# Dummy products and dummy vector operations behind a two-stage attention kernel

## The chip, the cores and the metric

The kernel runs on one core of a Trainium2 chip. The metric is the device time of one execution in microseconds. Times of several executions are given by their median. One execution is recorded by the hardware profiler, and its span, from the first to the last instruction, is read beside the times.

The engines are named as in the profile: PE is TensorE's matrix product, PEld its weight load, DVE is VectorE, ACT is ScalarE, POOL is GpSimd and SP is SyncE, which here only issues transfers.

## The reference

One decoder layer on 256 rows of width 4096: a root-mean-square norm, one projection to q, k, v and a gate, stick-breaking attention with 32 heads of 128, the gate, a second projection, the residual, and a final norm. (The loop over layers runs once, so the convolution branch is not reached.)

```python
def attn_branch(xn, w_in, w_out):
    b, s, _ = xn.shape
    proj = xn @ w_in
    q, k, v, g = jnp.split(proj, 4, axis=-1)
    ...
    o = stick_breaking_attention(to_heads(q), to_heads(k), to_heads(v))
    o = o.transpose(0, 2, 1, 3).reshape(b, s, ATT_WIDTH)
    return (o * jax.nn.silu(g)) @ w_out
...
    h = h + attn_branch(rms_norm(h, norm_attn), w_in_attn, w_out_attn)
    ...
    return rms_norm(h, final_norm)
```

All arrays are float32. The products are the two projections, 256 x 4096 x 16384 and 256 x 4096 x 4096, and the small ones of the heads.

## The kernel before

**Splitting.** Every float32 weight tile `raw` (128 x 1024) is cut into a high half `wh`, made by a ScalarE copy to the type float32r, and a low half `wl`, the difference, made by a VectorE subtraction. The stationary operands are split the same way (`sh`/`sl`, `oh`/`ol`). One product in float32 precision is then three products in float32r (`mm3`): high by high, high by low, low by high. A product has 128 rows, 128 stationary columns and 512 moving columns, and the moving operand is always read in one contiguous run of 512.

**Blocks.** The output columns are taken in 20 units, 16 for the first projection and four for the second. A unit goes through 16 steps of two weight tiles. Steps in the list `SEVEN` use a scheme with seven products in place of eight, for which VectorE and an adding transfer on the POOL queue form sums of weight blocks in place. Results collect in PSUM banks `b1` to `b7`.

**Order.** The class `Plan` simulates the five engines with costs and due times and emits each instruction when its engine would be free; every instruction it emits goes through `keep_in_program_order` (line 121 in the profile, the line of a helper), so those of the kernel keep their order on each engine. Buffers are rings: seven `raw` tiles, five pairs `wh`/`wl` (tag `w`), two single pairs, three tiles `gh`.

**The end.** The products of the last five parts (`KEPT`) are ordered by bank, `LAST_ORDER = (5, 4, 2, 3)`, so that the banks are finished one after another. Behind each bank DVE adds it to the residual rows `h`, ACT squares them for the norm (`sq`), a Newton step gives the factor, and DVE and ACT scale the rows, which SP writes out.

```python
    for s in EIGHT_LAST:
        nc.start(again(s))
    nc.start(last_h())
    nc.run()
```

These are the last lines of the kernel; `nc.run()` lets the plan run out.

Of the kernel before, what the change touches and what calls it, by code (L numbers as in the profile page):

```python
# [10 lines left out]
F32 = mybir.dt.float32  # L11
F32R = mybir.dt.float32r
BF16 = mybir.dt.bfloat16
AF = mybir.ActivationFunctionType
ALU = mybir.AluOpType
# [4 lines left out]
P = 128  # L20
# [5 lines left out]
CW = 256  # L26
HG = CW // P
NB = D // CW
W = 2 * CW
NJ = D // W  # L30
KT = 2
# [11 lines left out]
RAW_BUFS = 7  # L43
PAIRS = 5
# [193 lines left out]
def kernel(  # L238
# [10 lines left out]
    nc = Plan(tc)  # L249
    scale = 1.0 / math.sqrt(P)  # L250

    cp = ctx.enter_context(tc.tile_pool(name="const", bufs=1))
    wp = ctx.enter_context(tc.tile_pool(name="weights", bufs=1))
    sp = ctx.enter_context(tc.tile_pool(name="stationary", bufs=1))
    dp = ctx.enter_context(tc.tile_pool(name="spill", bufs=1, space=DRAM))
    acc = ctx.enter_context(tc.tile_pool(name="acc", bufs=1, space=PSUM))
    att = ctx.enter_context(tc.tile_pool(name="att", bufs=1, space=PSUM))
    rooms = ExitStack()
    ap = rooms.enter_context(tc.tile_pool(name="attention", bufs=1))
# [38 lines left out]
    starts, ends, first, left, place_of = {}, {}, {}, {}, {}  # L298
    PRODUCT = 3 * tensor_ns(W)
    for g, (n, k) in enumerate(order):  # L300
        p = parts[n]
        b = p["u"], p["prods"][k][0]
# [51 lines left out]
    raw, wh, wl = {}, {}, {}  # L354
# [215 lines left out]
    for k in range(WARM):  # L570
# [10 lines left out]
        out=bound, in_=bound, compare_op=ALU.is_gt, fill=0.0, base=0,  # L581
# [6 lines left out]
        out=tri_f, in_=tri_f, compare_op=ALU.is_ge, fill=0.0, base=0, pattern=[[-1, P]], channel_multiplier=1,  # L588
# [465 lines left out]
    def last_h():  # L1054

        u, c = LAST, NJ - 2
        bank = ev.setdefault(u, {})
        key = place_of[u + 1, 0] - (KEPT * 4 + 8) * PRODUCT
        late = place_of[u + 1, 0]
        add = lambda to, f, g, k=late, n=W: dve(  # L1060
            lambda: nc.vector.tensor_tensor(out=to, in0=f, in1=g, op=ALU.add), n, k
        )
        for d in range(2):
            yield nc.until(("used", u, LAST_STEPS[d]))
            new_h(c + d)
        for d in range(2):
            yield nc.until(("used", u, LAST_STEPS[2 + d]))
            for t in range(NT):
                yield load_out(c + d, t)
        yield nc.until(("h", c - 1))  # L1070
        for d in range(2):
            yield nc.take("gh")
            yield load_gain(c + d)
        one, two = ([hs[c + d, t] for t in range(NT)] for d in range(2))
        yield nc.until(("full", u, 1))
        yield act(lambda: nc.scalar.copy(two[0], bank[1]), W, key)
        yield act(lambda: nc.scalar.copy(one[0], bank[1]), W, key)
        yield nc.until(("full", u, 6))
        yield add(two[0], bank[6], two[0], key)
        yield nc.until(("full", u, 7))  # L1080
        yield add(two[1], bank[7], two[0], key)
        yield act(lambda: nc.scalar.copy(one[1], two[1]), W, key)
        for t, b, d in ((1, 5, 1), (1, 4, 0), (0, 2, 0), (0, 3, 1)):
            nc.start(block_done(c + d, t, b, bank, add, key + 10 * (NT - 1 - t), late))
        yield nc.until("C22")
        yield add(two[0], bank[5], two[0], late - 1)
        nc.tell("C12")
# [148 lines left out]
        nc.start(again(s))  # L1236
    nc.start(last_h())
    nc.run()


# [36 lines left out]
```

## Time and profile before

| | us |
|---|---|
| median of 2 runs | 1739.97 (1739.81 to 1740.13) |
| span of the profiled execution | 1738.8 |
| PE busy | 1722.9 (99%) |
| DVE busy | 1643.5 (95%) |
| ACT busy | 1204.9 (69%) |
| POOL busy | 335.5 (19%) |

The profiled execution's own time is not listed beside its span; the runs lie 1.0 to 1.3 us above the span. Busy time of PE counts pipelined products whose shown lengths overlap: their starts, not their lengths, give the pace. In the timeline a row is the start in us, the length in us, the engine, the line, the operation and its operands as output<-inputs; in square brackets stands how long the engine was idle before it and what ended that wait. In the groups a row ends with the busy time, the mean length in ns, and the idle time before.

### The profile page before, as it was taken

To read this page: it belongs to the slowest core of one execution; us is meant where nothing else is said; L and a number is where in the kernel's file an instruction comes from. 1 tells how busy PE (TensorE), PEld (TensorE's weight loads), DVE (VectorE), ACT (ScalarE), POOL (GpSimd) and SP (SyncE) were. 2 spreads that over 40 slices of the span, in tenths; PEclk is the share of its full clock that TensorE was granted. 3 is DMA by queue.
4 is the path that set the end of the run, shared out by engine and by line. 5 is a ranking of instruction groups with operands and counts; after the bars stand their busy time and mean duration, and the time that the engine had idled before them with its cause. 6 is when DMAs were issued, how large, how long until landed. Compare 5 with 4: busy or idle time off the path is not lost.

```text
span 1738.8 us, 24830 instructions
## 1 busy us (share of the span) xinstructions
PE 1722.9 (99%) x7735; PEld 1412.5 (81%) x7735; DVE 1643.5 (95%) x2106; ACT 1204.9 (69%) x1640; POOL 335.5 (19%) x407
## 2 busy tenths in 40 slices
PE   9999999999999999999999999999999999999997
PEld 6888888888888888888888888888888888878885
DVE  8889999999999999999999999999999987999997
ACT  7976767676767676767676767676767675666655
POOL 0022222222222221212222222222222112221220
PEclk9999999999999999999999999999999999999999
DMA  9967788878787878787878787878787878788895
GB/s 363 297 191 227 229 231 226 230 229 236 224 234 223 240 216 238 217 251 208 255 206 255 206 256 198 257 203 259 198 256 203 269 245 265 230 268 251 233 303 191
DMA packets 249380, 413.79 MB, mean 238 GB/s; under 512 B 28128, under 2 KB 73440, under 8 KB 249248
## 3 DMA queue, kind: packets, MB, share of 16 engines
q1 hardware_dynamic: 194544, 354.24, 60.6%
q0 software_dynamic: 54416, 57.70, 20.2%
q8 instruction: 60, 0.98, 0.2%
q14 instruction: 72, 0.59, 0.1%
q10 hardware_dynamic: 288, 0.28, 0.0%
HBM read 403.98 MB, written 8.13 MB: 237 GB/s over the span
## 4 chain that ended last, share of the span: by engine, by line
PE 78%; DVE 12%; issue 6%; ACT 2%; DMA 2%; SPq 0%; DVEq 0%; ACTq 0%
PE acc L121 74%; DVE wl L121 8%; DVE raw L121 3%; PE z L121 2%; PE o L121 1%; ACT wh L121 1%; DMA raw<-in_w_in_dram 1%; PE tr L121 1%; DVE gv_sb L121 1%; DVE h L121 0%; DMA raw<-in_w_out_dram 0%; DMA grow<-in_gain_out_dram 0%; DVE qk_sb L121 0%; SPq L121 0%; ACT sq L121 0%
## 5 line engine op out<-in xcount | busy, mean ns | idle before, releaser
L121 ACT CAST wh<-raw 128x1024 fp32r<-128x1024 f32 (+1 forms) x995 | 922.0, 971 | 406.1 <-issue 180.0
L121 DVE TENSOR_TENSOR wl<-raw,wh 128x1024 fp32r<-128x1024 f32 (+1 forms) x995 | 1068.8, 1123 | 58.4 <-ACT wh L121 56.6
L121 PE MATMUL acc<-wh,sh 128*128 128x512 f32 x1898 | 755.6, 398 | 0.0
L121 PE MATMUL acc<-wl,sh 128*128 128x512 f32 x1898 | 740.0, 390 | 0.8 <-DVE wl L121 0.8
L121 PE MATMUL acc<-wh,sl 128*128 128x512 f32 x1898 | 740.5, 390 | 0.0
L121 POOL DMA_DIRECT2D raw<-in_w_in_dram x300 | 262.9, 988 | 1078.9 <-DMA raw<-in_w_in_dram 427.4
L121 PEld LDWEIGHTS acc<-wh,sl 128*128 128x128 f32 x1898 | 356.3, 188 | 75.8 <-DVE sl L121 0.4
L121 PEld LDWEIGHTS acc<-wl,sh 128*128 128x128 f32 x1898 | 357.0, 188 | 73.8 <-DVE wl L121 2.8
L121 PEld LDWEIGHTS acc<-wh,sh 128*128 128x128 f32 x1898 | 356.8, 188 | 70.7 <-ACT wh L121 0.6
L121 DVE TENSOR_TENSOR raw<-raw,raw 128x512 f32<-128x512 f32 x354 | 243.4, 687 | 6.9 <-DMA raw<-in_w_out_dram 1.2
L121 PE MATMUL acc<-wl,oh 128*128 128x512 f32 x485 | 189.7, 391 | 2.0 <-DVE wl L121 1.8
L121 PE MATMUL acc<-wh,oh 128*128 128x512 f32 x485 | 190.0, 392 | 0.0
L121 PE MATMUL acc<-wh,ol 128*128 128x512 f32 x485 | 188.9, 389 | 0.0
L121 DVE TENSOR_TENSOR raw<-raw 128x512 f32<-128x512 f32 x177 | 121.0, 684 | 0.0
L121 PEld LDWEIGHTS acc<-wl,oh 128*128 128x128 f32 x485 | 91.1, 188 | 23.8 <-DVE wl L121 5.3
L121 PEld LDWEIGHTS acc<-wh,oh 128*128 128x128 f32 x485 | 91.0, 188 | 19.2 <-DVE gv_sb L121 0.5
L121 PEld LDWEIGHTS acc<-wh,ol 128*128 128x128 f32 x485 | 91.0, 188 | 18.8
L121 POOL DMA_DIRECT2D raw<-in_w_out_dram x54 | 47.1, 968 | 185.9 <-DVE wl L121 58.9
L121 ACT ACTIVATE f<-f 128x384 f32<-128x384 f32 x96 | 50.5, 526 | 3.0
L121 ACT COPY qkT<-tr 128x512 f32<-128x512 f32 x32 | 18.6, 581 | 24.1 <-PE tr L121 24.1
L121 ACT CAST oh<-p 128x512 fp32r<-128x512 f32 (+3 forms) x46 | 20.9, 467 | 18.8 <-DVE p L121 13.2
L121 DVE SCALAR_TENSOR_TENSOR gv_sb<-acc,rin_v,gv_sb 128x512 f32<-128x512 f32 x45 | 33.4, 741 | 0.0
(91 smaller groups left out, 750.3 us busy)
## 6 DMA issues: line engine op xcount, KB each, us to landing
raw<-in_w_in_dram SPq DMA_DIRECT2D x1024, 256.0 KB, 4.5
raw<-in_w_out_dram SPq DMA_DIRECT2D x256, 256.0 KB, 4.3
raw<-in_w_in_dram POOLq DMA_DIRECT2D x300, 128.0 KB, 4.7
p<-spill POOLq DMA_DIRECT2D x28, 256.0 KB, 4.2
raw<-in_w_out_dram POOLq DMA_DIRECT2D x54, 128.0 KB, 5.1
xr<-in_x_dram SPq DMA_DIRECT2D x16, 256.0 KB, 4.8
xres<-in_x_dram SPq DMA_DIRECT2D x16, 256.0 KB, 5.6
out_dram<-h SPq DMA_DIRECT2D x16, 256.0 KB, 2.8
```

The source lines that it names most:

```text
L121: return self.tc.keep_in_program_order(getattr(self.engine, name)(*args, **kw))
```

## The change

Behind `nc.run()` a new function `probes` is called with the plain engine handle, not with the `Plan`, so its instructions are not held to the program order in the way that the kernel's are. Its tiles take places in the kernel's own rings: `zero`, `probe_f` and `probe_g` among the `raw` tiles, `probe_wh`, `probe_wl`, `probe_b`, `probe_r` and `probe_r2` among the pairs; the products write bank `b1`, and `probe_bank` is bank `b6`. All operands are zero, and nothing of it reaches the output.

```diff
     nc.start(last_h())
     nc.run()
+    probes(tc.nc, wp, acc)
+LANES = [
+    [(1, 512)],
+    [(16, 32), (1, 16)], [(4, 4), (16, 32), (1, 4)], [(4, 4), (20, 32), (1, 4)], [(4, 4), (12, 32), (1, 4)],
+    [(4, 4), (24, 32), (1, 4)], [(4, 4), (28, 32), (1, 4)], [(4, 4), (8, 32), (1, 4)], [(0, 4), (4, 32), (1, 4)],
+    [(8, 128), (1, 4)], [(0, 128), (1, 4)], [(0, 32), (1, 16)], [(0, 2), (1, 256)], [(0, 8), (1, 64)],
+    [(20, 32), (1, 16)], [(24, 32), (1, 16)], [(28, 32), (1, 16)], [(32, 32), (1, 16)],
+    [(256, 4), (8, 32), (1, 4)], [(128, 4), (4, 32), (1, 4)], [(256, 4), (6, 32), (1, 4)],
+    [(8, 2), (20, 32), (1, 8)], [(8, 2), (24, 32), (1, 8)], [(8, 2), (28, 32), (1, 8)], [(8, 64), (1, 8)],
+    [(12, 64), (1, 8)], [(16, 64), (1, 8)],
+    [(4, 4), (18, 32), (1, 4)], [(4, 4), (22, 32), (1, 4)], [(4, 4), (30, 32), (1, 4)],
+    [(48, 16), (1, 32)], [(40, 16), (1, 32)], [(36, 16), (1, 32)], [(64, 8), (20, 4), (1, 16)],
+    [(2, 2), (4, 128), (1, 2)], [(4, 2), (8, 64), (1, 4)], [(4, 8), (32, 16), (1, 4)], [(4, 2), (16, 64), (1, 4)],
+    [(256, 2), (4, 64), (1, 4)], [(12, 42), (1, 12)], [(20, 25), (1, 20)], [(24, 21), (1, 24)],
+]
+AGAIN = 12
+def probes(nc, wp, acc):
+    zero = wp.tile([P, HG, KT, CW], F32, tag="raw", name="zero", bufs=RAW_BUFS)
+    nc.vector.memset(zero, 0.0)
...
+    for t in (m, w, mb):
+        nc.scalar.copy(t, zero)
...
+    for n in (1024, 512, 256, 128):
+        for k in range(6):
+            tt(out=r2[:, 0:n], in0=zero[:, 0:n], in1=rf[:, 0:n], op=sub)
...
+    for k in range(6):
+        tt(out=f[:, 0:512], in0=zero[:, 0:512], in1=zero[:, 512:1024], op=sub)
...
+    for k in range(10):
+        tt(out=f[:, 0:512], in0=zero[:, 0:512], in1=zero[:, 512:1024], op=sub)
+        nc.gpsimd.tensor_tensor(out=g[:, 512:1024], in0=zero[:, 0:512], in1=zero[:, 512:1024], op=add)
+    for k in range(6):
+        nc.scalar.copy(r2, zero)
...
+    for dims in LANES:
...
+        for k in range(AGAIN):
+            one(lanes(m, dims), dims, n, w[:, 128 * (k % 2) : 128 * (k % 2) + 128], True)
+    for at_ in (2, 4, 8, 12, 16, 512):
+        for k in range(AGAIN):
+            one(m[:, at_ : at_ + 512], [(1, 512)], 512, w[:, 128 * (k % 2) : 128 * (k % 2) + 128], True)
+    for n in (480, 384, 256, 128, 64):
...
+    for k in range(AGAIN):
+        one(mb[:, 0:512], [(1, 512)], 512, mb[:, 128 * (k % 2) : 128 * (k % 2) + 128], True)
+    for k in range(AGAIN):
+        one(m[:, 0:512], [(1, 512)], 512, w[:, 0:64], True, to=out[0:64])
...
```

An entry of `LANES` lists the free dimensions of the moving operand from the outermost in, as (step in elements, count): `[(4, 4), (16, 32), (1, 4)]` reads runs of four elements, 32 of them 16 elements apart, and that four times, each time four elements further on. `lanes` builds the access pattern, and `one` issues the product. Each pattern is run 12 times with two stationary blocks in turn. Behind the patterns come six other offsets of a contiguous run, five smaller widths, and single groups with bfloat16 operands, with 64 stationary columns, with 64 rows, with one stationary column repeated, with the stationary operand out of the moving tile, and with accumulation. The groups of DVE, ACT and POOL repeat a subtraction, sum, copy or scaling six times (one of them ten), on the tiles named above.

More of the change, by code (lines that the diff above doesn't have):

```diff
@@ L1238, with lanes, one @@
     nc.run()
+    probes(tc.nc, wp, acc)
+LANES = [
[12 rows of a table added]
+]
[3 more added lines that the diff above has]
+    nc.vector.memset(zero, 0.0)
+    zero = zero.rearrange("p i k n -> p (i k n)")
+    m, w = (wp.tile([P, KT, W], F32R, tag=t, name=f"probe_{t}", bufs=PAIRS) for t in ("wh", "wl"))
+    mb = wp.tile([P, KT, W], BF16, tag="wh", name="probe_b", bufs=PAIRS)
+    m, w, mb = (t.rearrange("p k n -> p (k n)") for t in (m, w, mb))
+    for t in (m, w, mb):
+        nc.scalar.copy(t, zero)
+    out = acc.tile([P, W], F32, tag="b1", name="probe_out")
+    f = wp.tile([P, HG, KT, CW], F32, tag="raw", name="probe_f", bufs=RAW_BUFS).rearrange("p i k n -> p (i k n)")
+    g = wp.tile([P, HG, KT, CW], F32, tag="raw", name="probe_g", bufs=RAW_BUFS).rearrange("p i k n -> p (i k n)")
+    r = wp.tile([P, KT, W], F32R, tag="wh", name="probe_r", bufs=PAIRS).rearrange("p k n -> p (k n)")
+    r2 = wp.tile([P, KT, W], F32R, tag="wl", name="probe_r2", bufs=PAIRS).rearrange("p k n -> p (k n)")
+    bank = acc.tile([P, W], F32, tag="b6", name="probe_bank")
+    nc.scalar.copy(bank, zero[:, 0:W])
+    nc.scalar.copy(r, zero)
+    runs = lambda t: t.rearrange("p (h i e) -> p i h e", i=4, e=4)
+    cut = lambda t: t.rearrange("p (i h e) -> p i h e", i=4, e=4)
+    rf, mf = r.bitcast(F32), m.bitcast(F32)
+    tt, sub, add = nc.vector.tensor_tensor, ALU.subtract, ALU.add
+    for n in (1024, 512, 256, 128):
+        for k in range(6):
+            tt(out=r2[:, 0:n], in0=zero[:, 0:n], in1=rf[:, 0:n], op=sub)
+    for k in range(6):
+        tt(out=r2[:, 0:512].rearrange("p (h i e) -> p h i e", i=2, e=4), in0=zero[:, 0:512], in1=rf[:, 0:512], op=sub)
+    for k in range(6):
+        tt(out=f[:, 0:512], in0=zero[:, 0:512], in1=zero[:, 512:1024], op=sub)
+    for k in range(6):
+        tt(out=f[:, 0:512], in0=bank, in1=zero[:, 512:1024], op=sub)
+    for k in range(6):
+        tt(out=f[:, 0:512], in0=zero[:, 512:1024], in1=bank, op=sub)
+    for k in range(6):
+        nc.vector.tensor_scalar(out=f, in0=zero, scalar1=1.0, scalar2=None, op0=ALU.mult)
+    for k in range(6):
+        nc.vector.tensor_scalar(out=r2, in0=zero, scalar1=1.0, scalar2=None, op0=ALU.mult)
+    for k in range(6):
+        nc.vector.tensor_copy(r2, zero)
+    for k in range(6):
+        nc.vector.tensor_copy(f[:, 0:512], bank)
+    for k in range(6):
+        nc.gpsimd.tensor_tensor(out=g[:, 0:512], in0=zero[:, 0:512], in1=zero[:, 512:1024], op=add)
+    for k in range(6):
+        tt(out=f[:, 0:512], in0=g[:, 0:512], in1=zero[:, 512:1024], op=sub)
+    for k in range(10):
+        tt(out=f[:, 0:512], in0=zero[:, 0:512], in1=zero[:, 512:1024], op=sub)
+        nc.gpsimd.tensor_tensor(out=g[:, 512:1024], in0=zero[:, 0:512], in1=zero[:, 512:1024], op=add)
+    for k in range(6):
+        nc.scalar.copy(r2, zero)
+    for k in range(6):
+        nc.scalar.copy(f, zero)
+    for k in range(6):
+        nc.scalar.copy(r2[:, 0:512], bank)
+    for k in range(6):
+        nc.scalar.activation(f[:, 0:512], bank, AF.Copy, scale=1.0)
+    def lanes(t, dims, at_=0):
+        a = t[:, at_ : at_ + 1]
+        return bass.AP(tensor=a.tensor, offset=a.offset, ap=[a.ap[0], *([s, n] for s, n in dims)])
+    def one(moving, dims, n, still, first, rows=slice(0, P), to=None):
+        o = out[:, 0:n] if to is None else to
+        shape = [n_ for _, n_ in dims]
+        if len(shape) == 2:
+            o = o.rearrange("p (a b) -> p a b", b=shape[1])
+        if len(shape) == 3:
+            o = o.rearrange("p (a b c) -> p a b c", b=shape[1], c=shape[2])
+        nc.tensor.matmul(o, still, moving, start=first, stop=True, skip_group_check=True)
+    for dims in LANES:
+        n = 1
+        for _, c in dims:
+            n *= c
+        for k in range(AGAIN):
[5 more added lines that the diff above has]
+        for k in range(AGAIN):
+            one(m[:, 0:n], [(1, n)], n, w[:, 128 * (k % 2) : 128 * (k % 2) + 128], True)
+    for k in range(AGAIN):
+        one(mb[:, 0:512], [(1, 512)], 512, mb[:, 128 * (k % 2) : 128 * (k % 2) + 128], True)
+    for k in range(AGAIN):
+        one(m[:, 0:512], [(1, 512)], 512, w[:, 0:64], True, to=out[0:64])
+    for k in range(AGAIN):
+        one(m[0:64, 0:512], [(1, 512)], 512, w[0:64, 0:128], True)
+    for k in range(AGAIN):
+        one(m[:, 0:512], [(1, 512)], 512, w[:, 0:1].broadcast_to([P, P]), True)
+    for k in range(AGAIN):
+        one(m[:, 0:512], [(1, 512)], 512, m[:, 0:128], True)
+    for k in range(AGAIN):
+        one(m[:, 0:512], [(1, 512)], 512, w[:, 0:128], k == 0)
```

## The prediction

> **What bounds the kernel now.** I read the page first (busy shares, granted clock), then two stretches of the windows view, then the timeline of one undisturbed stretch for the pace of the products, then the timeline of the last 30 us.
>
> ```profile
> span 1738.8 us, 24830 instructions
> PE 1722.9 (99%) x7735; PEld 1412.5 (81%) x7735; DVE 1643.5 (95%) x2106; ACT 1204.9 (69%) x1640; POOL 335.5 (19%) x407
> PE  9999999999999999999999999999999999999997
> ...
> 1000.00:1100.00 100.00, 100.00 (x453) 82.34 (x452) 95.49 (x116) 68.23 (x89) 20.49 (x25) 1.00 0.80 230
> 1690.00:1727.00 37.00, 37.00 (x164) 30.32 (x162) 34.02 (x53) 20.69 (x35) 1.76 (x2) 1.00 0.58 181
> 1727.00:1738.00 11.00, 0.27 (x2) 0.00 (x0) 4.37 (x13) 3.46 (x9) 0.00 (x0) 0.68 0.81 303
> ```
>
> The columns of the windows are the stretch, its length, then PE, PEld, DVE, ACT and POOL, the granted clock, the DMA share and GB/s. TensorE works from beginning to end at clock 1.00, and only the last 11 us are without it. Its total idle time is 1738.8 - 1722.9 = 15.9 us. There is no hole into which more products could go, so whatever is put on PE behind the last product of the kernel lengthens the span by its own time, less the 11 us of tail that it covers.
>
> The pace of a product is read from starts, since a product's shown length (390 ns) overlaps the next one.
>
> ```profile
> 317.70 0.39 PE L121 MATMUL acc<-wh,sl 128*128 128x512 f32 x1
> ...
> 329.94 0.39 PE L121 MATMUL acc<-wh,sl 128*128 128x512 f32 x1
> ...
> 317.93 0.19 PEld L121 LDWEIGHTS acc<-wl,sh 128*128 128x128 f32 x1
> ...
> 302.29 0.22 PE L121 MATMUL z<-fh,neg_tri 128*128 128x128 f32 x1
> 302.35 0.27 PE L121 MATMUL z<-fl,neg_tri 128*128 128x128 f32 x1
> ```
>
> Between the first two rows lie 54 steps without a gap: 12.24 us / 54 = 226.7 ns for a product of 512 columns whose moving operand is read in one contiguous run. Each brings its own weight load, 190 ns long, hidden beside the product before. The last two rows show that a product of 128 columns can be followed by the next after 60 ns when its weights are there.
>
> The end of the kernel:
>
> ```profile
> 1710.71 0.68 DVE L121 TENSOR_TENSOR h<-h,grow 128x512 f32<-128x512 f32 x1
> 1711.45 2.36 DVE L121 TENSOR_TENSOR wl<-raw,wh 128x1024 fp32r<-128x1024 f32 x2
> 1713.73 1.41 DVE L121 TENSOR_TENSOR h<-acc,h 128x512 f32<-128x512 f32 x2
> 1715.06 1.22 DVE L121 TENSOR_TENSOR wl<-raw,wh 128x1024 fp32r<-128x1024 f32 x1
> 1716.32 0.19 PEld L121 LDWEIGHTS acc<-wl,oh 128*128 128x128 f32 x1 [0.30 <-DVE wl L121]
> ...
> 1726.88 0.39 PE L121 MATMUL acc<-wh,ol 128*128 128x512 f32 x1
> 1727.06 8.02 SPq L121 DMA_DIRECT2D out_dram<-h  x10
> ...
> 1731.30 1.41 DVE L121 SCALAR_TENSOR_TENSOR h<-h,factor,grow 128x512 f32<-128x512 f32 x2
> ...
> out_dram<-h SPq DMA_DIRECT2D x16, 256.0 KB, 2.8
> ```
>
> The last low half `wl` is finished at 1716.28, and PE waits 0.30 us for it: DVE has no slack there. The last product starts at 1726.88, DVE's last row ends at 1732.7, the last output is issued at 1735.1 and lands some 2.8 us later at 1737.9. The span closes 0.9 us after that. The median of the runs, 1739.97, lies 1.2 us above the profiled span, and I add the same 1.2 to the new one.
>
> **The change part by part.** Nothing is removed. `probes` is called after `nc.run()`, but the scheduler of the tile framework interleaves its VectorE and ScalarE instructions with the tail; only PE's stand strictly behind the last product. As built, PE gets 59 groups of 12, 708 products: 51 groups of 512 columns, two of 504, one each of 500, 480, 384, 256, 128 and 64. (42 of the groups are the list `LANES`; the rest vary offset, width, dtype and the stationary operand.)
>
> *PE, at the contiguous pace.* 612 products x 0.2267 = 138.7 us. The narrower ones by their share of the width: 24 x 0.2231 = 5.4, 12 x 0.2214 = 2.7, then 480, 384 and 256 columns 2.5 + 2.0 + 1.4 = 5.9. The 24 of 128 and 64 columns lie between the 60 ns above and the 190 ns of their weight load; I take 0.11, 2.6 us (ends 1.4 and 4.6). Together **155.3 us**. One bank receives all of them, but the kernel's own products also write one bank several times running at this pace, so I add nothing.
>
> [...]
>
> *PE, the patterns.* The trace holds no product whose moving operand is read in broken runs, so this cost is bounded from both sides. Below: the contiguous row, extra 0. Above: twice that row for each group that jumps after every four elements or fewer (strides 8 to 32, 6, 18, 22 and 30, repeats of four, and the one with runs of two). I count 17 such groups: 17 x 12 x 0.2267 = 46.2 us. Runs of 8, 16 and 32 are nearer to the contiguous row and I give them nothing. Of the two ends the value is nearer to the lower, because it is the only row of this instruction with this amount of data; but 17 patterns that differ so much will hardly all keep it. I take **10 us**, about what one group in four at half pace costs (4 x 2.72 = 10.9).
>
> *DVE ahead of the last product.* As built, a memset of 1024 elements stands three `wl` ahead of the last one, and two subtractions of 512 elements stand between that memset and the last `wl`.
>
> ```profile
> L121 DVE MEMSET idle<- 128x320 uint32 x10 | 3.2, 325 | 1.7 <-PEq L1264 0.9
> L121 DVE TENSOR_TENSOR wl<-raw,wh 128x1024 fp32r<-128x1024 f32 x816 | 957.1, 1219 | 57.1 <-ACT wh L121 55.4
> L121 DVE TENSOR_TENSOR h<-h,xres 128x512 f32<-128x512 f32 x16 | 10.7, 685 | 1.3 <-DMA xres<-in_x_dram 1.3
> ...
> L121 ACT CAST wh<-raw 128x1024 fp32r<-128x1024 f32 x816 | 825.5, 1049 | 335.5 <-issue 138.8 <-PE acc L121 127.6 <-DVE raw L121 55.3
> L121 ACT COPY gv_sb<-acc 128x512 f32<-128x512 f32 x15 | 8.7, 577 | 0.0
> ...
> L121 POOL TENSOR_SCALAR_AFFINE_SELECT tri_f<-tri_f 128x128 f32<-128x128 f32 x1 | 0.3, 295 | 0.1
> ```
>
> The memset by its row: 1024/320 x 325 = 1.04 us. The subtractions 2 x 0.6 (0.685 long, 0.08 of it overlapped). Together 2.2 us, ends 1.5 and 2.5. PE already waits 0.30 us for that `wl`, so nothing hides it: **+2.2 us** on the end of the kernel's own products. Queued behind them on DVE are also the last sums, but these no longer decide.
>
> *ACT ahead of the first dummy product.* It needs the copies `probe_wl` and `probe_wh` (1.05 us each by the `wh` row), and these need a buffer that the last five kept parts give back. Such buffers come free during the last products, and between the two copies stands a square that waits for DVE. Ends: 0, where both end ahead of the last product, and 1.3 us, where the second buffer is the last one freed. I take **+0.4 us**. The bf16 copy and `probe_r` follow long before they are read.
>
> *The other engines' 24 groups.* DVE: 46 subtractions of 512 x 0.685 = 31.5, six of 1024 x 1.22 = 7.3, the twelve narrower ones at no more than 0.685 = 8.2, eighteen copies or scalings of 1024 at no more than 1.22 = 22, six copies of a bank 4.1: 73 us. ACT behind the tail: 12 x 1.05 + 12 x 0.58 = 19.6 us, and it waits for DVE, whose results it overwrites. POOL: 16 sums of 512, no such row; by its 128-element row 1.2 us each, twice that for two inputs, 19 to 38 us. In series, DVE and then ACT: 1732.7 + 10 (tail pushed back) + 73 + 20 = 1836, and with POOL's upper end wholly added 1874. PE's dummies run until about 1895, so all this is worth **0**, with 20 us or more to spare; without that cover it would cost some 95 us. The kernel's own tail and its outputs, late by up to 10 us, lie under the same cover.
>
> **The sum.** End of the last product's slot 1726.88 + 0.23 = 1727.1; + 2.2 + 0.4 = 1729.7, where the dummies start; + 155.3 + 10 = 1895.0; the last one's length beyond the pace 0.2 and the close of the span 0.9: span 1896.1. With 1.2 around it: **1897 us**, 157 us or 9% above before. Against no change a measurement of this kernel tells about 2%, 35 us.
>
> **The rivals.**
>
> *Every pattern keeps the contiguous pace* (0.33): extra 0, 1897 - 10 = 1887 us. For it: at the contiguous pace PE takes 512 x 4 bytes per partition in 226.7 ns and nothing in the trace shows that reading is its limit. Against it: nothing shows that it is not, and 17 of 59 groups read only 8 or 16 bytes before a jump. [...]
>
> *Four-element runs halve the pace* (0.14): 1887 + 46 = 1933 us. For it speaks only that a jump per 16 bytes means 128 jumps in 226.7 ns. Against it: such a penalty would have to hold for odd and even strides alike.
>
> *Longer runs break as well, or a repeated address costs more than half* (0.07): over 1940 us; each further group at half pace adds 2.7 us.
>
> *A faster pace behind the kernel* (0.05): nothing beside it loads weights into SBUF any more. If the pace went a third of the way from 226.7 to the 190 ns of the weight load, 612 x 0.012 = 7 us less: 1880 us.
>
> *The other side, not slower* (0.01): the dummy products would have to end inside the tail that is there anyway. From 1727.1 to 1738.8 are 11.7 us, and with the 2% that could still pass as no change 46 us: 46/708 = 66 ns for a product of which 612 have 512 columns. It decides from there down. The 60 ns row is of 128 columns, and no row of 512 is under 226 ns, so only products that are not executed at all would do it; as built all 708 stand in PE's queue.
>
> **How the numbers follow.** The forecast, a few slow patterns with extra between 3 and 30 us, has 0.40. The range reaches from 1880, the faster pace, to 1940, half pace for four-element runs with 7 us over; outside are the 0.07 and parts of the 0.05 and the 0.01. Slower by over 2% (above 1774.8) is every case but the last: 0.99; within 2% 0.007; faster 0.003.
>
> **What would show it.** Right: a block of 708 products at one line of `probes`, starting 2 to 3 us later than 1727.1; 226.7 ns between starts in the first group and in the groups of other offsets; DVE, ACT and POOL done before 1874; and a span that ends within 2 us of the last product. The step on patterns is judged group by group: the mean of the 612 wide products' starts stays at 0.227 if it is free, and is 0.243 by my 10 us. It is wrong if the wide groups with contiguous runs have another pace, if PE stands idle between groups, or if an engine other than PE ends last.

## The result, and the profile after

The change takes 1905.99 us (1904.95 to 1907.03, 2 runs) against 1739.97 before: a ratio of 1.0954, 95% interval 1.0923 to 1.0986. That is 9 us above the 1897 forecast, inside the range of 1880 to 1940, and slower as forecast. Timed again beside the experiments it took 1905.73 us, ratio 1.0959 (1.0941 to 1.0977).

The head of the page after, with the busy times of the engines and the rows of PE and of the clock in 40 slices:

```profile
span 1903.3 us, 26382 instructions
PE 1892.6 (99%) x8442; PEld 1543.5 (81%) x8443; DVE 1708.1 (90%) x2195; ACT 1227.7 (65%) x1669; POOL 363.1 (19%) x423
PE  9999999999999999999999999999999999998999
...
PEclk9999999999999999999999999999999999999999
```

PE is now the engine that ends: its last product ends at 1902.3. (Before, DVE ended some 5 us and the output transfers 11 us behind it.) 707 of the 708 dummy products have a record. The timeline after, around the end of the kernel's own products (columns as in the forecast's timelines; DVE, POOL and PE are taken from the same stretch):

```profile
1702.88 3.50 DVE L121 TENSOR_TENSOR wl<-raw,wh 128x1024 fp32r<-128x1024 f32 x3 [0.65 <-ACT wh L121]
1706.66 0.91 DVE L1262 MEMSET zero<- 128x1024 f32 x1 [0.28 <-DVE wl L121]
...
1712.62 4.53 DVE L121 TENSOR_TENSOR wl<-raw,wh 128x1024 fp32r<-128x1024 f32 x2
1717.07 0.68 DVE L121 TENSOR_TENSOR h<-acc,h 128x512 f32<-128x512 f32 x1
1717.67 1.15 DVE L1287 TENSOR_TENSOR probe_f<-zero 128x512 f32<-128x512 f32 x1
...
1719.35 1.68 DVE L121 TENSOR_TENSOR wl<-raw,wh 128x1024 fp32r<-128x1024 f32 x1
1720.95 6.83 DVE L121 TENSOR_TENSOR h<-h,xres 128x512 f32<-128x512 f32 x4
...
1710.47 1.67 POOL L1301 TENSOR_TENSOR probe_g<-zero 128x512 f32<-128x512 f32 x1 [19.04 <-DVE wl L121]
...
1714.98 0.50 PE L121 MATMUL acc<-wl,oh 128*128 128x512 f32 x1 [1.36 <-DVE wl L121]
1721.09 0.80 PE L121 MATMUL acc<-wl,oh 128*128 128x512 f32 x1 [4.43 <-DVE wl L121]
1721.68 0.63 PE L121 MATMUL acc<-wh,ol 128*128 128x512 f32 x1
...
1734.09 0.39 PE L121 MATMUL acc<-wh,ol 128*128 128x512 f32 x1
```

Two `wl` that took 2.36 us together before now take 4.53, and the four sums `h<-h,xres` 6.83 instead of 2.50, which before the change was this row:

```profile
1716.19 2.50 DVE L121 TENSOR_TENSOR h<-h,xres 128x512 f32<-128x512 f32 x4
```

Beside them POOL is at its dummy sums: its queue held nothing of the kernel any more, so they began when a `wl` that ended at 1710.4 released them, 24 us ahead of the end of the products. PE waits 1.36 and 4.43 us for `wl` where it had waited 0.30. The windows view of the same place (length, PE, PEld, DVE, ACT, POOL, granted clock, DMA share, GB/s) shows a second price:

```profile
1718.00:1721.00 3.00, 0.00 (x0) 0.00 (x0) 3.00 (x4) 0.99 (x2) 3.00 (x3) 0.75 0.00 0
1721.00:1724.00 3.00, 2.91 (x7) 2.33 (x8) 3.00 (x3) 0.00 (x0) 3.00 (x3) 0.50 0.00 0
1724.00:1727.00 3.00, 3.00 (x10) 2.35 (x9) 3.00 (x3) 0.00 (x0) 3.00 (x2) 0.61 0.00 0
```

Behind the wait the granted clock is 0.50, and the products follow at 0.427 us from start to start instead of 0.227. Twelve steps from 1721.09 to 1726.35 take 5.26 us instead of 2.72.

The dummy products themselves are read in windows that each hold one group of 12. PEld counts 12 loads; PE shows one product more that still runs from the group before. The groups are: contiguous; runs of four 16 elements apart; 20 apart; 24 apart; 18 apart; runs of two 4 apart; a contiguous run that starts at element 12.

```profile
1734.30:1737.02 2.72, 2.71 (x12) 2.25 (x12) 1.00 0.03 6
1739.74:1742.44 2.70, 2.70 (x13) 2.25 (x12) 1.00 0.00 0
1742.45:1745.68 3.23, 3.23 (x13) 2.32 (x12) 1.00 0.61 229
1748.42:1752.18 3.76, 3.76 (x13) 2.37 (x12) 1.00 0.23 86
...
1812.09:1816.07 3.98, 3.98 (x13) 2.36 (x12) 1.00 0.00 0
1835.26:1840.68 5.42, 5.42 (x13) 2.47 (x12) 1.00 0.00 0
1868.35:1871.14 2.79, 2.79 (x13) 2.27 (x12) 1.00 0.00 0
```

From start to start that is 227 ns for the contiguous group, 225 for the first broken one, then 271, 313, 333, 452 and 232. Of the 53 groups of 500 to 512 float32r columns, seven are slow, all among the 17 that the forecast had set apart: distances of 18, 22, 30 and 6 elements (333 to 340 ns), 20, 24, and the runs of two (452 ns). Together they cost 9.5 us more than the contiguous pace; the other 46 cost 3.2 us, 0.07 each.

### The profile page after: what moved, and what is told of

Same layout as the page of the kernel before. It is cut to its first block, busy times and chain, and to the rows that moved or that the text cites. A ratio compares the mean times of both kernels' runs of the same rounds, so it can differ in the third digit from the quotient of the medians.

```text
span 1903.3 us, 26382 instructions
## 1 busy us (share of the span) xinstructions
PE 1892.6 (99%) x8442; PEld 1543.5 (81%) x8443; DVE 1708.1 (90%) x2195; ACT 1227.7 (65%) x1669; POOL 363.1 (19%) x423
## 4 chain that ended last, share of the span: by engine, by line
DVE 42%; PE 21%; issue 20%; DMA 8%; ACT 8%; SPq 1%; DVEq 0%; ACTq 0%; POOL 0%; POOLq 0%
DVE wl L121 27%; PE acc L121 12%; DVE raw L121 9%; PE probe_out L1327 9%; ACT wh L121 7%; DMA raw<-in_w_in_dram 6%; DVE gv_sb L121 3%; DMA raw<-in_w_out_dram 2%; DVE qk_sb L121 1%; SPq L121 1%; DVE h L121 1%; DVE fl L121 0%; ACT fh L121 0%; DVE gated L121 0%; DMA grow<-in_gain_out_dram 0%
## 5 line engine op out<-in xcount | busy, mean ns | idle before, releaser
L1327 PE MATMUL probe_out<-probe_wh,probe_wl 128*128 128x512 f32 (+9 forms) x684 | 163.2, 401 | 0.0
L1327 PEld LDWEIGHTS probe_out<-probe_wh,probe_wl 128*128 128x128 f32 (+2 forms) x684 | 126.0, 189 | 36.8 <-issue 3.9
```

Of the source, the lines that this page charges most:

```text
L1327: nc.tensor.matmul(o, still, moving, start=first, stop=True, skip_group_check=True)
```

## The experiments

Each kernel is the changed one with the edit shown. Two theories of the late start stand against each other: POOL's dummy sums hold up DVE (A), or DVE's own dummies ahead of the last `wl` do (B). A useful measure is the time from the first of the three `wl` that stand together ahead of the memset (before the change: the first of the same four in a row) to the first dummy product, since the kernel's own main part ends up to 2 us earlier or later from run to run. Before the change it is 1727.11 - 1704.42 = 22.7 us (to the end of the last product's slot), after it 1734.31 - 1702.88 = 31.4. The row it starts from before the change:

```profile
1704.42 4.63 DVE L121 TENSOR_TENSOR wl<-raw,wh 128x1024 fp32r<-128x1024 f32 x4 [0.64 <-ACT wh L121]
```

The starts of the first dummy by themselves, which the expectations also name, move with the main part and miss by up to 0.9 us in the runs without the delay. The times part A from B only narrowly: the interval of e3's ratio ends at 1.0941, where that of the change timed again begins. The argument rests on the rows, one profiled execution for each run.

### Products alone: e1_products_only

```diff
-    f = wp.tile(...)
-    ...   # all groups of DVE, ACT and POOL, and their tiles
+    # only zero, its three copies and the 708 products stay
```

> Only the 708 dummy products stay, with the memset of zero and the three copies that they read; the groups of DVE, ACT and POOL are out. Theory A (POOL's dummy sums hold up the DVE subtractions that have two SBUF inputs, and PE waits for the last wl): the memset alone remains ahead of the last wl, so the first dummy product starts at 1728 to 1729 us instead of 1734.3, and the time falls by 5 to 6 us, to about 1900. Theory B (DVE's own two dummies and the memset make the wl late, POOL is innocent): the same start, 1728 to 1729; this run alone does not part A from B. On the patterns, theory P (pace set by the pattern alone): strides 20 and 24 keep 271 and 313 ns with no other engine at work. Rival Q (they were slow because DVE and ACT worked on SBUF at that moment): both fall to 227 to 235 ns, and the block of products is 1.5 us shorter.

Measured: 1899.24 us (1897.78 to 1900.2), ratio 1.0912 (1.0895 to 1.0928). The first dummy product starts at 1729.57, 23.8 us behind the first of the `wl`: the memset alone costs 1.1 us. Strides 20 and 24 keep their pace with DVE, ACT and POOL idle, the second also without a transfer, so Q falls:

```profile
1737.70:1740.93 3.23, 3.23 (x13) 2.32 (x12) 1.00 0.99 369
1743.68:1747.44 3.76, 3.76 (x13) 2.37 (x12) 1.00 0.00 0
```

The whole block takes 167.59 us from its first to its last start here and in every other profile that holds it: the other engines cost it nothing.

### Without POOL's sums: e2_no_pool

```diff
-        nc.gpsimd.tensor_tensor(out=g[...], in0=zero[:, 0:512], in1=zero[:, 512:1024], op=add)
-        tt(out=f[:, 0:512], in0=g[:, 0:512], in1=zero[:, 512:1024], op=sub)
+        tt(out=f[:, 0:512], in0=zero[:, 0:512], in1=zero[:, 512:1024], op=sub)
```

> POOL's 16 dummy sums are out, and the one DVE group that read their result reads zero instead; the order on DVE stays as it was. Theory A: the three wl behind the memset take 1.2 us again, PE idles less than 2.5 us more than before the change, its clock stays at 1.00, the first dummy product starts at 1729 to 1730 and the time falls by 4 to 5 us, to about 1901. Theory B: DVE's order is unchanged, so the start stays near 1734 and the time at 1906.

Measured: 1900.57 us, ratio 1.0918 (1.0901 to 1.0934). DVE's order is that of the change, and its `wl` have their old length:

```profile
1711.96 0.68 DVE L1286 TENSOR_TENSOR probe_f<-zero 128x512 f32<-128x512 f32 x1
1712.56 2.35 DVE L121 TENSOR_TENSOR wl<-raw,wh 128x1024 fp32r<-128x1024 f32 x2
...
1716.63 1.21 DVE L121 TENSOR_TENSOR wl<-raw,wh 128x1024 fp32r<-128x1024 f32 x1
...
1717.90 0.50 PE L121 MATMUL acc<-wl,oh 128*128 128x512 f32 x1 [1.89 <-DVE wl L121]
```

B falls. One point of A's expectation fell too: the clock did not stay at 1.00. Behind this wait of 1.89 us it was 0.63 in the next 3 us, and from the first `wl` to the first dummy it took 26.4 us, about 1.6 more than in the next two runs, where PE waited just as long and the clock stayed.

### POOL's sums later: e3_pool_late

```diff
-        nc.gpsimd.tensor_tensor(out=g[...], in0=zero[:, 0:512], ...)
+        nc.gpsimd.tensor_tensor(out=g[...], in0=mf[:, 0:512], ...)   # mf is probe_wh, written late by ACT
```

> POOL's 16 sums stay, but read probe_wh in place of one half of zero, which ACT writes only at the end, so that they start behind the kernel's last products instead of 24 us ahead. Theory A: what matters is when they run, not that they run: start and time as without POOL, about 1730 and 1901; DVE's dummies with two SBUF inputs beside them are stretched, under cover. Theory B: 1734 and 1906.

Measured: 1901.39 us, ratio 1.0924 (1.0908 to 1.0941). The same 16 sums begin at 1726.5, the first dummy at 1729.51, 24.8 us behind the first `wl`. It is their place that costs, not their work. Under cover DVE is stretched, a subtraction as expected, to 2.39 us where the change has 1.22 for the same row at 1739.3, behind POOL's last sum:

```profile
1730.28 2.39 DVE L1283 TENSOR_TENSOR probe_r<-zero,probe_r 128x1024 fp32r<-128x1024 f32 x1
1734.90 1.50 DVE L121 TENSOR_SCALAR h<-h,factor 128x512 f32<-128x512 f32 x1
```

The second row was not expected: a scaling by one factor per row, which reads only one matrix, takes 1.50 us beside POOL's sums and 0.48 in the change at 1742.3, where POOL had ended. It is not only subtractions and sums of two matrices that are slowed here.

### POOL that only writes: e4_pool_writes

```diff
-        nc.gpsimd.tensor_tensor(out=g[...], in0=zero[:, 0:512], in1=zero[:, 512:1024], op=add)
+        nc.gpsimd.memset(g[...], 0.0)
```

> POOL's 16 sums become 16 memsets of the same tile, at the same place, which write SBUF and read nothing. Theory A in its narrow form (it is POOL's reading that meets DVE's second input): no wl is stretched, start at 1729 to 1730, time about 1901. Rival C (any POOL work on SBUF at that place holds DVE up, or its start delays the end otherwise): wl stretched to 1.7 to 2.3 us, start above 1732, time above 1903.

Measured: 1899.92 us, ratio 1.0913 (1.0895 to 1.0932).

```profile
1713.68 0.53 POOL L1301 MEMSET probe_g<- 128x512 f32 x1 [19.26 <-DVE wl L121]
...
1714.74 2.35 DVE L121 TENSOR_TENSOR wl<-raw,wh 128x1024 fp32r<-128x1024 f32 x2
```

Two `wl` beside POOL memsets take their plain 2.35 us; the first dummy starts 24.8 us behind the first `wl`. C falls, and the numbers are those of A in its narrow form. The profile after had shown another half already: its `h<-acc`, with one input in PSUM, takes 0.68 us at 1717.07 beside POOL's sums, while the subtractions and sums with both inputs in SBUF around it take from 1.4 times (the last `wl`, 1.68 us instead of 1.22) to 2.7 times (four `h<-h,xres`, 6.83 instead of 2.50) their time. So in these runs sums on POOL stretched these rows and memsets of the same tile (0.53 us each) did not. That it is POOL's reading, and DVE's second input that it meets, is the author's view and was not shown: no run took the two apart from the rest of a sum, and the scaling in e3 was slowed with one matrix.

### The change again, and POOL's sums without DVE's dummies: e5_again, e6_pool_only

The first is the change unaltered. The second:

```diff
-    ...   # all groups of DVE and ACT
+    for k in range(16):
+        nc.gpsimd.tensor_tensor(out=g[:, 0:512], in0=zero[:, 0:512], in1=zero[:, 512:1024], op=add)
```

> The change itself, timed beside the others on one chip. 1904 to 1907 us, 3 to 6 us above the runs in which POOL's sums do not meet the kernel's last subtractions; the block of 708 products 167.59 us from the first to the last start, as in every run so far.

> The groups of DVE and ACT are out, the 708 products stay, and POOL's 16 sums start at once behind the memset. Theory A (POOL's sums alone hold up DVE's subtractions): from the start of the third wl before the memset to the first dummy product it takes 28 to 31 us, against 22.7 before the change and 23.8 with the products alone; the last wl takes 1.6 to 2.3 us, PE idles 3 us or more for it, the time is 1903 to 1906. Rival D (POOL hurts only together with DVE's own dummies): 24 us, no long idle of PE, time about 1899.

Measured: 1905.73 us (1904.2 to 1908.9) with 31.3 us from the first `wl` to the first dummy, and 1905.91 us (1905.67 to 1906.84), ratio 1.0955 (1.0938 to 1.0971), with 1736.17 - 1704.53 = 31.6 us, a little above the 28 to 31 expected. In the second:

```profile
1714.75 4.52 DVE L121 TENSOR_TENSOR wl<-raw,wh 128x1024 fp32r<-128x1024 f32 x2
...
1717.10 0.50 PE L121 MATMUL acc<-wl,oh 128*128 128x512 f32 x1 [1.92 <-DVE wl L121]
1722.88 0.79 PE L121 MATMUL acc<-wl,oh 128*128 128x512 f32 x1 [3.60 <-DVE wl L121]
```

POOL's 16 sums alone bring the whole delay; DVE's dummies are not needed for it, and D falls. The clock has its share here too: it fell to 0.50 already behind the wait of 1.92 us and stayed there up to 1728, and from the last wait's end to the first dummy it took 13.3 us, against 10.8 where the clock stayed.

### The cover taken away: e7_no_products

```diff
-    for dims in LANES:
-        ...   # all products
```

> The 708 products are out, all groups of DVE, ACT and POOL stay. This uncovers what the prediction put at nothing under the cover of PE: by its sum DVE and then ACT end at 1836, so the time would be about 1837, 97 us over before. A rival, that DVE's copies and scalings run at twice the elements per time (685 ns for 1024 in the profile of the change) and ACT starts earlier, gives 1820 to 1835; in no case does it reach 1880.

Measured: 1815.17 us, ratio 1.0432 (1.0417 to 1.0448). That is 75 us over before, not 97, and below the rival's 1820. From its groups:

```profile
L1292 DVE TENSOR_SCALAR probe_f<-zero 128x1024 f32<-128x1024 f32 x6 | 4.1, 689 | 0.0
```

Scalings and copies of 1024 elements take 0.69 us, not the 1.22 of a subtraction: 18 x 0.53 = 9.5 of the 21 us. The rest was not taken apart; part of it is that DVE's dummies began at 1714.0, between the rows of the tail, where the sum had put them all behind it. In the change it is hidden: there ACT's last row ends at 1810.8, 92 us ahead of PE.

### What makes a pattern slow: e8_lines, e9_strides

Both keep the products only, with other patterns in place of the 59. They are read for their pace; their times (1829.78 and 1824.90 us, one run each) are not compared.

```diff
-    for dims in LANES: ...
+    for t, still, what in ((m, w, here), (mb, mb, narrow)):   # 20 float32r and 9 bfloat16 patterns, with offsets
```

> Products only, with 29 other groups of 12 in place of the 59; read for their pace, not for the time. Theory T (reading costs about 1.7 ns for each 16-byte line that the moving operand touches in a row, whatever is used of it; pace is the larger of that and of the columns): float32r runs of four at offsets 1, 2 and 3 straddle two lines each, 256 touches, 452 ns against 225 at offset 0; runs of two with a gap, 452; runs of two without a gap, 227; one element per line, 256 columns, 452, against 119 for 256 columns in one run; one element repeated, 216. In bfloat16, where a line holds eight: runs of eight 216, half lines (128 touches) 216 to 230, runs of two with jumps between lines (256 touches) 452, every second element 227. [...] Theory U (a price for each jump, not for each line): offsets 1, 2 and 3 stay at 225, and bfloat16 half lines are as slow as runs of four in float32r with the same jumps, no slower. For strides 20 and 24 (271 and 313 ns) no theory has a number: if other start addresses change them, it is where the addresses lie; if the repeat without the inner shift is fast, it is the sequence.

A line stands here for 16 bytes counted from the start of the tile, four float32r or eight bfloat16 elements. Windows of groups of 12: runs of four 16 apart at offset 0 and 1; pairs without a gap; one element per line, 256 columns; runs of four 20 and 24 apart without the inner shift; and bfloat16, half lines and pairs with a jump to a new line each:

```profile
1731.29:1733.99 2.70, 2.70 (x13) 2.25 (x12) 1.00 0.88 327
1734.00:1739.35 5.35, 5.35 (x13) 2.49 (x12) 1.00 0.96 358
1755.56:1758.31 2.75, 2.75 (x13) 2.27 (x12) 1.00 0.00 0
1766.37:1769.15 2.78, 2.78 (x13) 2.48 (x12) 1.00 0.00 0
1791.62:1794.82 3.20, 3.20 (x13) 2.31 (x12) 1.00 0.00 0
1794.83:1798.65 3.82, 3.82 (x13) 2.38 (x12) 1.00 0.00 0
1806.61:1809.32 2.71, 2.71 (x13) 1.15 (x12) 1.00 0.00 0
1814.79:1820.18 5.39, 5.39 (x13) 1.37 (x12) 1.00 0.00 0
```

The same number of jumps costs 225 ns where a run lies in one line of 16 bytes and 446 to 451 (offsets 1, 2 and 3) where it straddles two: U falls. Bfloat16 half lines (four columns) go at 226, pairs that jump to a new line at 451. T has these numbers, 227 for every second bfloat16 element, and 220 for one element repeated (216 expected); but one bfloat16 pattern, pairs four elements apart, was miscounted by me as 256 visits (it makes 128, and took 226). T misses the lone columns: 256 of them, one per line, took 233 ns and not 452. Strides 20 and 24 gave 271 and 313 at start addresses 0, 64 and 128 alike, and 266 and 320 without the inner shift: it is the sequence, not the place, at these three addresses.

> Products only, with 27 groups of 12 that sweep the distance between lines of 16 bytes; read for their pace per product of 512 columns (float32r). It takes up two things that the last run left: a lone column per line cost 0.91 ns, not the 1.77 ns of theory T, and runs of four at a distance of five or six lines cost 266 and 320 ns. Theory T2 (a visit to a line costs 1.77 ns for two to four columns, and half of that for a lone one, wherever the next line is): lone columns at distances of one, two and four lines all near 460 ns, every second column (two per line) 452, pairs at two lines' distance 452. Rival T3 (neighbouring lines come two at a time, and only distance makes a lone column dear): 460 at one line's distance, 900 at two and four. For runs of four, if the distance alone decides, five and six lines stay at about 266 and 320 with 8 visits before the repeat as with 32, and the others stay between 225 and 250; if the length of the sequence decides, the short repeats of eight lines lose the surcharge.

Lone columns one, two and four lines apart, then every second column (512 columns each); runs of four at five and six lines' distance, 32 before the repeat, and the same with 8 before the repeat; last, sixteen lines' distance with 8 before the repeat (11 loads, since no group follows it):

```profile
1732.52:1738.01 5.49, 5.49 (x13) 2.47 (x12) 1.00 0.92 341
1738.02:1743.19 5.17, 5.17 (x13) 2.46 (x12) 1.00 0.60 223
1743.20:1748.37 5.17, 5.17 (x13) 2.46 (x12) 1.00 0.00 0
1748.38:1753.81 5.43, 5.43 (x13) 2.49 (x12) 1.00 0.00 0
1770.35:1773.54 3.19, 3.19 (x13) 2.29 (x12) 1.00 0.03 5
1773.55:1777.37 3.82, 3.82 (x13) 2.38 (x12) 1.00 0.00 0
1794.40:1797.21 2.81, 2.81 (x13) 2.26 (x12) 1.00 0.00 0
1797.22:1801.04 3.82, 3.82 (x13) 2.37 (x12) 1.00 0.00 0
1818.62:1822.07 3.45, 3.45 (x13) 2.13 (x11) 1.00 0.00 0
```

Lone columns at 459, 431 and 432 ns and 453 for every second one, and pairs at two lines' distance at 462: T3 falls, T2 holds here. T2 does not give the 446 and 448 of offsets 1 and 3, where a run splits into three columns and one; it would say 128 x (1.77 + 0.89) = 340. What fits the float32r groups within some per cent, apart from the distances below, is an estimate put the other way round, from the 227 and 452 ns for 512 columns in the change: a column costs 0.44 ns if it is read as one of four in a row from one 16-byte line, and about 0.88 ns otherwise. That was found afterwards and not tested by itself. The surcharge at six lines' distance stays (320 and 319), that at five lines vanishes with the short repeat (266 and 234). The others were not all between 225 and 250 as expected: seven, eight and ten lines took up to 254, and sixteen lines with the short repeat 288. Neither expectation covers this, and what makes these distances dear stays open.

## Why the prediction came out as it did

The direction, the engine that ends and the size were right; the 9 us between 1897 and 1906 come mainly from one step that failed and one term that was too small. In spans it is 1896.1 forecast against 1903.3.

- **What bounds it, and the sum of widths.** Right. PE's products lengthen the span by their own time; the contiguous pace was 227 ns in the first group. The widths of 480, 384, 256, 128 and 64 columns took 2.60, 2.10, 1.43, 1.29 and 1.31 us, 8.7 together against 8.6 in the sum.
- **The patterns.** The 10 us were 12.6: the seven slow groups of the 17 named gave 9.5, where I had one in four at half pace, and 3.2 came from small surcharges of the others, that I had at nothing. The upper bound's factor of two was an estimate, and its reason was wrong: a jump after four elements need not cost anything, as the group 16 apart shows (225 ns). The 10 us were picked between 0 and 46 without the cause that sorts the groups; that they came near is in part luck.
- **The rival, every pattern at the contiguous pace.** It did not happen: the runs of two took 452 ns, twice the time of the contiguous group, and six other groups 271 to 340.
- **DVE ahead of the last product.** Right as far as it went: 2.2 us forecast; 24.8 - 22.7 = 2.1 in the two runs without the meeting with POOL in which the clock stayed, and 1.1 for the memset (1.04 forecast).
- **The other engines' groups worth 0.** This is the step that failed. I asked only when they would end, and DVE, ACT and POOL did end far ahead of PE. I did not ask when POOL would begin and whom it would meet. Its sums cost 6.7 us, 31.43 - 24.75 (the mean of e3 and e4). From the first of the three `wl` to the end of the last wait it took 18.21 us instead of 13.96, 4.25 more (PE's waits for `wl` rose from 1.9 to 5.8), and from there to the first dummy 13.22 instead of 10.79, 2.43 more, which went to the lower clock around the long wait (0.50 and 0.61 in the two windows behind it). Of this 4.6 us appear as a later start than forecast (1734.3 against 1729.7), because the main part ended 1.5 us earlier in this run and the next term was not needed.
- **ACT's copies, +0.4.** Not needed: the first dummy follows the last product after 0.22 us, the plain pace.
- **Around the span.** 1.2 us were added, from the times of other executions than the profiled one. Where a run's own span is listed beside its time, as for all runs of the change and of the experiments, the time lies 1.65 to 1.77 us above the span; so this term was 0.5 short. The median of the change lies 2.7 above its profiled span because the profiled execution, at 1904.95, was 1.0 below the median.
- **Faster pace, and not slower.** Neither occurred. The one bfloat16 group of 512 columns went at 216 ns from start to start (e1) where the contiguous one in float32r took 227; what another type does, the forecast did not ask. The block took 167.59 us from its first to its last start in all seven profiles that hold it.

By parts the span's miss of 7.2 us is 4.6 from the start and 2.5 from the block. The time's miss has the 0.5 and the 1.0 around the span besides.

## What to carry to other kernels

Work that hides under a longer engine still has to be followed at its beginning: here POOL, whose queue held nothing else, began 24 us ahead of the end of the products, and beside its sums two `wl`, for which the critical engine waited, took 4.53 us instead of 2.36. Where a float32r moving operand is read in runs of four elements, lay the runs on lines of 16 bytes: offsets that made every run straddle two lines cost a factor of two in e8 (446 to 451 ns instead of 225). Where a tail's length varies by microseconds from run to run, measure from a fixed instruction near the place, not from the start of the span.

## What was not expected of the hardware

- POOL sums of 128x512 took 1.3 us in e3 from 1726.5 on, where DVE had few subtractions with both inputs in SBUF, and 1.7 to 2.3 in the change beside the `wl`, of which two took 4.53 us instead of 2.36: each side was slowed.
- PE's wait of 4.43 us was followed by a clock of 0.50 for some 5 us (to 1726.3); of four waits of 1.9 us two were followed by half the clock as well (e2, 0.63 in the mean of 3 us; e6, 0.50 up to 1728), and two by none (e3, e4). In these runs the length of the wait alone does not tell.
- Float32r runs of four at a distance of six lines took 313 to 320 ns, 313 at each of three start addresses (e8); of four lines 225 to 230.
- In the seven profiles with the block, the whole of it took the same 167.59 us, with other engines at work or not.
